# The first 8 MB of a streaming row sum: one load, or two half loads from two issuing engines

## The chip, the cores and the metric

The kernel runs on one core of one Trainium2 chip. The metric is the device time of one execution in microseconds (us). The span in a profile is some 1.4 us shorter than that execution's time (159.6 against 160.96 us for the kernel before).

Engines in the profile: ACT is ScalarE, DVE is VectorE, POOL is GpSimd, SP is SyncE, which only issues DMAs here. SPq and ACTq are the issuing instructions of SyncE and ScalarE. TensorE isn't used.

## The reference

```python
x = np.random.randn(32, 512, 1024).astype(np.float32)   # 67.11 MB
relu_x = np.maximum(x, 0)
return np.sum(relu_x, axis=-1).astype(np.float32)       # 64 KB
```

## The kernel before

The input is cut into eight portions of 16 rows on each of 128 partitions, 8.389 MB each. Seven are loaded whole into three buffers in turn, the eighth in smaller loads at the end. In the early portions ScalarE clamps a whole tile in place and VectorE sums its rows; towards the end both do single rows with clamp and sum in one instruction. `TWO` lists the row groups of each portion that are clamped and then summed. Lines that only count loads and semaphores are cut here.

```python
ROWS = 16
NBUF = 3
TWO = [[16], [16], [16], [8, 8], [8, 8], [7, 7], []]
# ...
def load(dst, src, after=None):
    dma = nc.sync.dma_start(out=dst, in_=src)
    if after:
        dma.wait_op(sems.dve, after[1], "sem-ge")     # the sum that frees the buffer
    dma.then_inc(sems.loads[n_load], 16)
# ...
for j in range(NB):
    buf = bufs[j % NBUF]
    loaded = load(buf[:, :, :], rows(m, ROWS), j >= NBUF and freed[j - NBUF])
    c = 0
    act_waits = dve_waits = loaded
    for n in TWO[j]:
        clamp(buf[:, c : c + n, :], act_waits)        # ScalarE, Relu in place
        total(buf[:, c : c + n, :], m + c, n)         # VectorE, sum of each row
        act_waits = None
        c += n
    # ... single rows of the later portions
    freed.append((n_act, n_dve))
```

A last function takes away the barrier that opens a program and moves the first load to the front, so that it is SyncE's first instruction (`EARLY = 1`).

Of the kernel before, what the change touches and what calls it, by code (L numbers as in the profile page):

```python
# [9 lines left out]
ROWS = 16  # L10
NBUF = 3


TWO = [[16], [16], [16], [8, 8], [8, 8], [7, 7], []]
ACT = [0, 0, 0, 0, 0, 2, 9]
DVE = [0, 0, 0, 0, 0, 0, 7]

# [2 lines left out]
TAIL = [8, 4]  # L20
START_PIECE, END_PIECE = 280, 260
PIECES = [240, 244]

EARLY = 1


def kernel(tc: tile.TileContext, x: bass.AP, out: bass.AP):
    nc = tc.nc
    sems = Semaphores(tc)

    tc.close()
    tc.compile()
    nc.cur_bb = nc.bb_map[tc.start_bb_name]
    body = nc.cur_bb.bb.instructions
    ends = list(body)
    body.clear()
    n_stores = relu_sum(nc, sems, x, out)
    body.extend(ends)


    nc.cur_bb = nc.bb_map[tc.start_bb_name + "_end"]
    nc.cur_bb.bb.instructions.clear()
    nums = sorted(s.num for s in (*sems.loads, sems.act, sems.dve))
    cleared = range(nums[0], nums[-1] + 1)
    assert len(cleared) == len(nums)
    nc.sync.sem_clear(cleared)
    nc.sync.wait_ge(sems.stored, 16 * n_stores).then_inc(sems.stored, -16 * n_stores)
    open_without_barrier(tc, EARLY)


class Semaphores:
    def __init__(self, tc: tile.TileContext):
        n = len(TWO) + len(TAIL) + 2 + len(PIECES)
        self.loads = [tc.alloc_semaphore(f"load{i}") for i in range(n)]
        self.act = tc.alloc_semaphore("act")
        self.dve = tc.alloc_semaphore("dve")
        self.stored = tc.alloc_semaphore("stored")


def relu_sum(nc, sems: Semaphores, x: bass.AP, out: bass.AP):  # L60
    x_flat = x.flatten_outer_dims()
    N, D = x_flat.shape
    NT = N // P
    NB = len(TWO)
    assert N == P * NT == P * ROWS * (NB + 1)
# [19 lines left out]
    def rows(m, n):  # L85
        if m < ROWS:
            return xf[:, m : m + n, :]
        return xv[:, m - ROWS : m - ROWS + n, :]
# [5 lines left out]

    n_load = n_act = n_dve = n_store = 0

    def load(dst, src, after=None):
        nonlocal n_load
        dma = nc.sync.dma_start(out=dst, in_=src)  # L99
        if after:  # L100
            dma.wait_op(sems.dve, after[1], "sem-ge")
        dma.then_inc(sems.loads[n_load], 16)
        n_load += 1
        return sems.loads[n_load - 1]
# [10 lines left out]
    def clamp(ap, loaded):  # L115
        nonlocal n_act
        i = nc.scalar.activation(out=ap, in_=ap, func=RELU)  # L117
        if loaded is not None:
            i.wait_op(loaded, 16, "sem-ge")
        i.then_inc(sems.act, 1)  # L120
        n_act += 1

    def total(ap, m, n):
        nonlocal n_dve
        nc.vector.tensor_reduce(  # L125
            out=res[:, m : m + n], in_=ap, axis=mybir.AxisListType.X, op=ADD
        ).wait_op(sems.act, n_act, "sem-ge").then_inc(sems.dve, 1)
        n_dve += 1

    def act_row(ap, accum_out, loaded):  # L130
        nonlocal n_act
        i = nc.scalar.activation(out=ap, in_=ap, func=RELU, accum_out=accum_out)  # L132
        if loaded is not None:
            i.wait_op(loaded, 16, "sem-ge")
        i.then_inc(sems.act, 1)
        n_act += 1

    def dve_row(ap, accum_out, loaded):
        nonlocal n_dve
        i = nc.vector.tensor_scalar(  # L140
            out=ap,
            in0=ap,
            scalar1=0.0,
            scalar2=None,
            op0=MAX,
            op1=ADD,
            accum_out=accum_out,
        )
        if loaded is not None:
            i.wait_op(loaded, 16, "sem-ge")  # L150
        i.then_inc(sems.dve, 1)
        n_dve += 1

    freed = []
    m = 0
    for j in range(NB):
        buf = bufs[j % NBUF]
        loaded = load(buf[:, :, :], rows(m, ROWS), j >= NBUF and freed[j - NBUF])
        c = 0
        act_waits = dve_waits = loaded  # L160
        for n in TWO[j]:
            clamp(buf[:, c : c + n, :], act_waits)
            total(buf[:, c : c + n, :], m + c, n)
            act_waits = None
            c += n
        for _ in range(ACT[j]):
            act_row(buf[:, c, :], res[:, m + c : m + c + 1], act_waits)
            act_waits = None
            c += 1
        for _ in range(DVE[j]):  # L170
            dve_row(buf[:, c, :], res[:, m + c : m + c + 1], dve_waits)
            dve_waits = None
            c += 1
        assert c == ROWS
        freed.append((n_act, n_dve))
        m += ROWS


    buf = bufs[NB % NBUF]
    c = 0  # L180
    for n in TAIL:
        loaded = load(
            buf[:, c : c + n, :], rows(m, n), None if c else freed[NB - NBUF]
        )
        for i in range(n):
            if i % 2 == 0 or (n == 8 and i == 7):
                act_row(buf[:, c, :], res[:, m : m + 1], loaded if i == 0 else None)
            else:
                dve_row(buf[:, c, :], res[:, m : m + 1], loaded if i == 1 else None)
            c += 1  # L190
            m += 1

    flat = buf[:, :, :].rearrange("p c d -> p (c d)")
    src = rows(m, 4).rearrange("p c d -> p (c d)")
    at = c * D
# [3 lines left out]
    last, w = parts[-1], PIECES[-1]  # L199
    others = [last[:, w + i : w + i + 1] for i in range(extra)]  # L200
    loaded = load(flat[:, at : at + b], src[:, :b])
    act_row(buf[:, c, :], res[:, m : m + 1], loaded)
    sums_act = n_act
# [3 lines left out]
    loaded = load(flat[:, at + end : at + 4 * D], src[:, end:])  # L207
# [13 lines left out]
    for i in range(len(PIECES) - 1):  # L221
# [3 lines left out]
        out=last[:, :],  # L225
# [9 lines left out]
    return n_store  # L235


def open_without_barrier(tc: tile.TileContext, n_loads: int):



    SP = mybir.EngineType.SP
    blocks = tc.nc.main_func.blocks
    opening = blocks[0].instructions
    body = next(b for b in blocks if b.name == tc.start_bb_name).instructions
    for i in list(opening):
        if isinstance(i, (mybir.InstDrain, mybir.InstEventSemaphore)):
            opening.remove(i)
    loads = [i for i in body if i.engine == SP][:n_loads]
    for i in loads:  # L250
        assert isinstance(i, mybir.InstDMACopy)
        body.remove(i)
    at = next(n for n, i in enumerate(opening) if i.engine == SP)
    opening[at:at] = loads


# [28 lines left out]
```

## Time and profile before

| | before |
|---|---|
| time, median of 6 runs | 161.07 us (160.96 to 161.15) |
| span of the profiled run | 159.6 us |
| DMA packets, share of 16 engines' span | 98.0% |
| VectorE busy, ScalarE busy | 74%, 65% |
| start of the clamps of loads 1, 2, 3 | 21.87, 41.19, 60.55 us |

How to read it: a clamp that starts just as its load lands, after a long idle time of ScalarE, is a mark for the landing. If the marks stand evenly 19.35 us apart, the stream of bytes has no gap, and only what lies ahead of the stream and behind it can be changed without moving fewer bytes. The prediction shows these lines.

### The profile page before, as it was taken

What the parts mean: (1) busy time and instruction counts of PE and PEld (TensorE: products, weight loads), DVE (VectorE), ACT (ScalarE), POOL (GpSimd) and SP (SyncE); (2) the same over time, 40 slices, a digit from 0 to 9 for tenths busy, and PEclk for the clock granted to TensorE, in tenths of its full rate; (3) what the DMA queues carried; (4) which work ended last, traced back from release to release, by engine and by line L of the source; (5) the groups of instructions that cost most, each with busy time, mean ns of one, the idle gap of its engine ahead of it and who ended that gap; (6) DMA issues with size and microseconds to landing.
All of it is one profiled execution on the core that took longest, in us unless ns stands there. A gap on an engine that the chain in (4) does not pass through costs nothing.

```text
span 159.6 us, 120 instructions
## 1 busy us (share of the span) xinstructions
DVE 117.6 (74%) x43; ACT 104.2 (65%) x50; POOL 0.2 (0%) x4
## 2 busy tenths in 40 slices
DVE  0000000009999499994999999999999999999986
ACT  3000059990699708996099951999329993499995
POOL 0000000000000000000000000000000000000000
DMA  7996996996997999979979969969969969798993
GB/s 279 509 526 263 526 526 263 526 509 279 526 476 312 526 394 394 526 345 443 526 328 460 526 263 526 526 263 526 509 279 526 493 296 526 337 452 382 418 412 119
DMA packets 2304, 67.18 MB, mean 421 GB/s; under 512 B 640, under 2 KB 896, under 8 KB 1024
## 3 DMA queue, kind: packets, MB, share of 16 engines
q1 hardware_dynamic: 2304, 67.18, 98.0%
HBM read 67.11 MB, written 0.07 MB: 421 GB/s over the span
## 4 chain that ended last, share of the span: by engine, by line
DMA 43%; DVE 34%; ACT 17%; another core or an unknown queue 3%; SPq 1%; issue 0%
DMA io<-in_x_dram 43%; DVE res L125 32%; ACT io L117 17%; DVE io L140 1%; SPq L99 1%; DVE piece L224 0%; DVE piece L140 0%
## 5 line engine op out<-in xcount | busy, mean ns | idle before, releaser
L125 DVE TENSOR_REDUCE res<-io 128x8 f32<-128x8192 f32 (+2 forms) x9 | 101.1, 11287 | 40.0 <-ACT io L117 40.0
L117 ACT ACTIVATE io<-io 128x8192 f32<-128x8192 f32 (+2 forms) x9 | 81.7, 9110 | 47.7 <-DMA io<-in_x_dram 47.7
L132 ACT ACTIVATE io<-io 128x1024 f32<-128x1024 f32 x20 | 20.9, 1045 | 6.0 <-DMA io<-in_x_dram 6.0
L140 DVE TENSOR_SCALAR_CACHE_REDUCE io<-io 128x1024 f32<-128x1024 f32 (+2 forms) x15 | 15.8, 1110 | 0.5 <-DMA io<-in_x_dram 0.4
L132 ACT ACTIVATION_READ_ACCUMULATOR io<-io 128x1 f32 x20 | 3.8, 188 | 0.0
L117 ACT ACT_TABLE_LOAD x1 | 1.3, 1283 | 0.1
L140 DVE DVE_READ_ACCUMULATOR io<-io 128x1 f32 x15 | 1.2, 82 | 0.0
L224 DVE TENSOR_SCALAR_CACHE_REDUCE piece<-piece 128x247 f32<-128x247 f32 x1 | 0.4, 410 | 0.0
L140 DVE TENSOR_SCALAR_CACHE_REDUCE piece<-piece 128x240 f32<-128x240 f32 x1 | 0.4, 397 | 0.0
L269 POOL MEMSET const-bfloat16-1.0<- 128x1 bf16 x1 | 0.1, 101 | 0.0
L269 POOL MEMSET const-uint8-127<- 128x1 uint8 x1 | 0.1, 101 | 0.0
L269 POOL MEMSET const-float32-0.0<- 128x1 f32 x1 | 0.1, 98 | 0.2 <-issue 0.2
L269 POOL MEMSET const-float32-1.0<- 128x1 f32 x1 | 0.1, 98 | 0.0
L224 DVE DVE_READ_ACCUMULATOR piece<-piece 128x1 f32 x1 | 0.1, 83 | 0.0
L140 DVE DVE_READ_ACCUMULATOR piece<-piece 128x1 f32 x1 | 0.1, 82 | 0.0
## 6 DMA issues: line engine op xcount, KB each, us to landing
io<-in_x_dram SPq DMA_DIRECT2D x1, 4096.0 KB, 21.6
io<-in_x_dram SPq DMA_DIRECT2D x1, 2048.0 KB, 26.1
io<-in_x_dram SPq DMA_DIRECT2D x1, 1164.0 KB, 28.4
io<-in_x_dram SPq DMA_DIRECT2D x1, 642.0 KB, 29.5
piece<-in_x_dram SPq DMA_DIRECT2D x1, 122.0 KB, 29.2
piece<-in_x_dram SPq DMA_DIRECT2D x1, 120.0 KB, 29.4
io<-in_x_dram SPq DMA_DIRECT2D x7, 26.9
out_dram<-res SPq DMA_DIRECT2D x1, 55.0 KB, 1.6
```

The costliest lines, as they stand in the source:

```text
L99: dma = nc.sync.dma_start(out=dst, in_=src)
L117: i = nc.scalar.activation(out=ap, in_=ap, func=RELU)
L125: nc.vector.tensor_reduce(out=res[:, m : m + n], in_=ap, axis=mybir.AxisListType.X, op=ADD).wait_op(sems.act, n_act, "sem-ge").then_inc(se ...
L132: i = nc.scalar.activation(out=ap, in_=ap, func=RELU, accum_out=accum_out)
L140: i = nc.vector.tensor_scalar(out=ap, in0=ap, scalar1=0.0, scalar2=None, op0=MAX, op1=ADD, accum_out=accum_out,)
L224: nc.vector.tensor_scalar(out=last[:, :], in0=last[:, :], scalar1=0.0, scalar2=None, op0=MAX, op1=ADD, accum_out=res[:, NT - 2 : NT - 1],) ...
L269: nc = _bacc.Bacc("TRN2", target_bir_lowering=False, num_devices=1)
```

## The change

The first portion comes as two loads of 8 rows a partition, one issued by SyncE and one by ScalarE, each moved to the front of its engine's program. The two halves are clamped and summed separately. The intent: start the transfer from two places at once, and start computing on half of the data. The core of the diff (counts of semaphores and unchanged lines cut):

```diff
-TWO = [[16], [16], [16], [8, 8], [8, 8], [7, 7], []]
+TWO = [[8, 8], [16], [16], [8, 8], [8, 8], [7, 7], []]
...
-EARLY = 1
+HALF = 8
...
-    def load(dst, src, after=None):
+    def load(dst, src, after=None, by=nc.sync):
         nonlocal n_load
-        dma = nc.sync.dma_start(out=dst, in_=src)
+        dma = by.dma_start(out=dst, in_=src)
...
-        loaded = load(buf[:, :, :], rows(m, ROWS), j >= NBUF and freed[j - NBUF])
+        if j == 0:
+            loaded = load(buf[:, :HALF, :], rows(m, HALF))
+            other = load(buf[:, HALF:, :], rows(m + HALF, ROWS - HALF), by=nc.scalar)
+        else:
+            loaded = load(buf[:, :, :], rows(m, ROWS), j >= NBUF and freed[j - NBUF])
+            other = None
...
-            act_waits = None
+            act_waits, other = other, None
...
-    loads = [i for i in body if i.engine == SP][:n_loads]
-    for i in loads:
-        assert isinstance(i, mybir.InstDMACopy)
-        body.remove(i)
-    at = next(n for n, i in enumerate(opening) if i.engine == SP)
-    opening[at:at] = loads
+    for engine in (mybir.EngineType.SP, mybir.EngineType.Activation):
+        first = next(i for i in body if isinstance(i, mybir.InstDMACopy) and i.engine == engine)
+        body.remove(first)
+        at = next(n for n, i in enumerate(opening) if i.engine == engine)
+        opening.insert(at, first)
```

## The prediction

> **What bounds the kernel now.** I began with the chain that ended last and the busy table of the page. They show DVE 74% busy, ACT 65%, and a chain that jumps between loads, clamps and sums. That chain must not be taken at its word, so the next view was the DMA queue, then the order of time for ACT and DVE, then how many bytes the DMA engines took up in short windows at the start.
>
> From the page (the queue, then the chain as shares of the span):
>
> ```profile
> DVE 117.6 (74%) x43; ACT 104.2 (65%) x50; POOL 0.2 (0%) x4
> q1 hardware_dynamic: 2304, 67.18, 98.0%
> DMA 43%; DVE 34%; ACT 17%; another core or an unknown queue 3%; SPq 1%; issue 0%
> ```
>
> The second line says that packets fill 98.0% of 16 DMA engines' whole span. No compute engine comes near that.
>
> From the timeline (start, duration, engine and line, what it did, and in brackets the idle time before it with what ended it):
>
> ```profile
> 21.87 13.86 ACT L117 ACTIVATE io<-io 128x16384 f32<-128x16384 f32 x1 [20.47 <-DMA io<-in_x_dram]
> 35.76 17.22 DVE L125 TENSOR_REDUCE res<-io 128x16 f32<-128x16384 f32 x1 [35.76 <-ACT io L117]
> 41.19 13.86 ACT L117 ACTIVATE io<-io 128x16384 f32<-128x16384 f32 x1 [5.46 <-DMA io<-in_x_dram]
> 55.08 17.22 DVE L125 TENSOR_REDUCE res<-io 128x16 f32<-128x16384 f32 x1 [2.10 <-ACT io L117]
> 60.55 13.86 ACT L117 ACTIVATE io<-io 128x16384 f32<-128x16384 f32 x1 [5.50 <-DMA io<-in_x_dram]
> ...
> 118.60 12.24 ACT L117 ACTIVATE io<-io 128x7168 f32<-128x7168 f32 x2 [5.40 <-DMA io<-in_x_dram]
> ...
> 137.96 1.06 ACT L132 ACTIVATE io<-io 128x1024 f32<-128x1024 f32 x1 [5.04 <-DMA io<-in_x_dram]
> ```
>
> ACT waits about 5.5 us for every 8 MB load, and its starts mark the landings: 21.87, 41.19, 60.55. The steps are 19.32 and 19.36, and from 118.60 to 137.96 again 19.36. A load is 128 x 16 x 1024 x 4 bytes = 8.389 MB, so the stream runs at 8.389 MB / 19.35 us = 433.5 GB/s without a gap. The input is 67.11 MB, eight such portions, 154.8 us. The span is 159.6 us, so 4.8 us are outside the stream: 21.84 - 19.35 = 2.5 us ahead of it, and about 2.3 us behind it (last sums, store).
>
> The DMA row of the chain, 28.43 us from 126.91 to 155.34, holds mostly queueing: that load was issued when a sum of rows ended at 126.04, while the load before it was still on its way until 137.9. Its wait had 11.9 us to spare. For the fourth load the same: it waits for the sum that ends at 35.76 + 17.22 = 52.98, and the third load lands only at 60.5, 7.5 us later. So no buffer wait ever starves the queue.
>
> The start, in windows (width, DVE, ACT, POOL busy, clock, DMA packet time per engine as a share of the window and counted at the packet's start, GB/s likewise):
>
> ```profile
> 0.00:1.00 1.00, 0.00 (x0) 0.88 (x1) 0.20 (x4) 1.00 0.00 0
> 1.00:2.00 1.00, 0.00 (x0) 0.40 (x1) 0.00 (x0) 1.00 3.01 1049
> 2.00:3.50 1.50, 0.00 (x0) 0.00 (x0) 0.00 (x0) 1.00 0.00 0
> 3.50:5.00 1.50, 0.00 (x0) 0.00 (x0) 0.00 (x0) 1.00 1.61 699
> 5.00:6.00 1.00, 0.00 (x0) 0.00 (x0) 0.00 (x0) 1.00 0.00 0
> 6.00:7.00 1.00, 0.00 (x0) 0.00 (x0) 0.00 (x0) 1.00 2.42 1049
> ```
>
> 1049 GB/s in a window of 1 us is 1.049 MB, exactly 16 packets of 64 KB, one for each DMA engine. So all first packets start between 1.0 and 2.0 us and last 3.01 us on average; the second ones, between 3.5 and 5.0 us, last 1.61 x 1.5 = 2.42 us, and the third ones 2.42 us too. From the packet records the first 64 KB packet starts at 1.01 us, the sixteenth at 1.81, the mean at 1.24; the second packets start at 3.96 to 4.58. So the 2.5 us ahead of the stream are some 1.24 us until the mean engine has data to move, 3.01 - 2.42 = 0.59 us of a slow first packet, 4.58 - 4.25 = 0.33 us by which the slowest engine trails the mean (the starts of the last engine trail the mean just so in all later rows), and about 0.3 us until the last semaphore is seen.
>
> **What the Trainium skill says.** "DMA: Bandwidth & Descriptors", section "Issuing engines are not separate DMA queues": DMAs from different engines run on the same 16 DMA engines and interleave; using several saves only the time to initiate them. Here an issue takes 0.38 us on SyncE (its first row in the chain), and nothing yet shows two queues at once. The same page, "Queues, rings and completion order": each DMA engine goes round-robin between the queue rows at packet granularity, so two halves issued together should end together and not one after the other; the trace of before has one queue and can't say. Same page, "Where 436 GB/s comes from": a ceiling of 435.2 GB/s at the SBUF ports, with about 358 named as binding for HBM reads; the trace disagrees with the second and comes within 0.4% of the first at 433.5. Same page, "Latency and other measured facts": first byte after about 600 ns on this path; here the first packet starts 1.01 us after the issue begins, of which 0.38 is the issue, which leaves 0.63 and agrees.
>
> **The change part by part.**
>
> *Two half loads in place of the first.* The bytes are the same, 4.19 MB each, and so is the stream's rate. The packets are 32 KB, an estimate of 1.21 us each at the present rate. They alternate between the rings on every engine. SyncE's own next load (8 MB) stands behind its half, so no engine runs dry. I expect both halves to land at nearly the same time, around 20.5 to 22 us. Nothing is gained in the stream itself: 0.
>
> *Time to the first packet.* SyncE's load already was the first instruction of the program, so its first packet stays at about 1.0 us: 0. ScalarE's earliest work now is a table load at 0.12 us; its DMA takes that place, so its half is queued about 0.1 us after SyncE's. It costs ACT some 0.4 us and pushes the 1.28 us table load to an end near 1.9 us, 19 us before its first clamp: off the path.
>
> *The slow first packet and the engine lag.* This is the one place with something to win, at most 0.59 + 0.33 = 0.92 us. A second ring may overlap the slow opening with the other ring's, or the two rings may both have slow first packets in turn (up to another 0.59 us lost). I choose a gain of 0.15 us, a small part of the first, as nothing in the trace says what the 0.59 us are.
>
> *First buffer's compute.* One clamp of 13.86 us becomes two of 7.02 (the later 8-row ones last that long; two together 13.95), one sum of 17.22 becomes two of 8.68. The first sum can start at 21.9 + 7.0 = 28.9 in place of 35.8, the second ends near 46.2 in place of 52.98. That frees the first buffer about 6.8 us earlier and the fourth load is issued so much earlier, but it then waits behind the third load till 60.5 as before. DVE idles up to 55.1 in both. Gain: 0.
>
> *Semaphore.* One more to clear at the end: under 0.1 us.
>
> Sum: 161.07 - 0.15 = 160.9 us. As every later landing comes so much earlier, ACT and DVE behind it shift as a whole: DVE runs without a break from 74.44, which was itself released by the clamp of the load that landed at 60.5.
>
> **Rivals.** *The earlier sum as a real gain.* Speaking for it: 6.8 us of DVE waiting vanish, and the chain gives DVE 34%. Against it: the DMA row of 98.0% and 7.5 us of spare time at the buffer's wait. If it were right the time would be near 154 us, but 154.8 us of stream alone forbid that. *Starting the stream much sooner.* Even if all 2.5 us before it vanished, the time would be 158.6, 1.6% less; that bounds the gain under 2%. A full removal of slow packet and lag gives 160.2. *Interference of two queues.* If alternating rings or 32 KB packets cost 5% of the first 19.35 us, the time rises by 1.0 us to 162.0; 2% slower (3.2 us) would need 17% there. Against it: the tail of the kernel has small packets too and the windows from 147.0 to 155.3 still show 415 GB/s. *A late ScalarE queue.* If its half came 5 us late, only the second clamp would wait, and DVE has 9 us to spare: the time stays.
>
> **Range and chances.** The effect I count is 0.15 us, with a possible 0.9 us each way where the start is unclear; runs of the same kernel spread by 0.1 us. So 160.3 to 161.5 should hold it 8 times in 10. Beyond 2% either way, no mechanism that I found reaches: 1% for faster, 1% for slower, left for what I can't see.
>
> **What would show it.** Right: packets of the first 8 MB on two queues, 32 KB each; first ones at about 1.0 us; the two halves land within some 1.5 us of each other near 21.5; ACT still waits over 5 us for each 8 MB load with landings 19.35 us apart; DVE's first sum near 29 us; the buffer's third use still without effect on landings; the queue still 98%. Wrong: landings after the first that have moved by over 0.6 us against before, a step between landings other than 19.35, first packets well before 1.0 us, or a longer time with the stream unchanged, which would be a cost ahead of the first or behind the last instruction.

## More of the kernel before

All runs here are of state fast, with a granted clock of 1.0.

The experiments were taken on three chips, each time with the kernel before beside them (its medians were 161.09, 161.03 and 161.06 us).

## The result, and the profile after

The changed kernel takes 161.09 us (160.95 to 161.21, 6 runs) against 161.07 us of the kernel before, ratio 1.0001 with a 95% interval of 0.9988 to 1.0014: the same. A ratio here is the mean time of one kernel's fast runs over that of the other's of the same rounds, so it is not quite the ratio of the medians that are quoted.

The queues on the page of the changed kernel (queue, kind, packets, MB, share of 16 engines' span):

```profile
q1 hardware_dynamic: 2304, 62.98, 91.9%
q10 hardware_dynamic: 144, 4.19, 6.1%
```

ScalarE's half is 4.19 MB on a queue of its own; the sum of the shares, 98.0%, is that of before.

The timeline of the changed kernel's start:

```profile
0.12 0.37 ACTq L100 DMA_DIRECT2D io<-in_x_dram  x1
...
0.52 1.28 ACT L118 ACT_TABLE_LOAD   x1 [0.52 <-issue]
21.80 13.95 ACT L118 ACTIVATE io<-io 128x8192 f32<-128x8192 f32 x2 [20.00 <-DMA io<-in_x_dram]
28.87 17.28 DVE L126 TENSOR_REDUCE res<-io 128x8 f32<-128x8192 f32 x2 [28.87 <-ACT io L118]
41.17 13.86 ACT L118 ACTIVATE io<-io 128x16384 f32<-128x16384 f32 x1 [5.41 <-DMA io<-in_x_dram]
55.05 17.22 DVE L126 TENSOR_REDUCE res<-io 128x16 f32<-128x16384 f32 x1 [8.91 <-ACT io L118]
60.51 13.86 ACT L118 ACTIVATE io<-io 128x16384 f32<-128x16384 f32 x1 [5.49 <-DMA io<-in_x_dram]
...
118.57 12.24 ACT L118 ACTIVATE io<-io 128x7168 f32<-128x7168 f32 x2 [5.40 <-DMA io<-in_x_dram]
...
137.92 1.06 ACT L133 ACTIVATE io<-io 128x1024 f32<-128x1024 f32 x1 [5.03 <-DMA io<-in_x_dram]
```

The first sum starts at 28.87 us in place of 35.76, and the first buffer's sums end at 28.87 + 17.28 = 46.15 in place of 52.98. But the clamp of the second load starts at 41.17 in place of 41.19, and so on down to 137.92 in place of 137.96. VectorE's gain went into a longer idle time: 8.91 us before the sum at 55.05, where it was 2.10.

The same is to be read in SyncE's waits for VectorE (total, how often, the longest). First the kernel before, then the changed one:

```profile
SPq L99 <- DVE res L125: 123.3, 5, 51.7
```

```profile
SPq L100 <- DVE res L126: 123.3, 5, 44.8
```

The longest wait, that of the fourth load for the first buffer, is 6.9 us shorter. The total is 123.3 us in both: what SyncE wins at its first wait it spends at the next ones, as the sums behind are bound to landings that haven't moved.

The windows of the changed kernel's start (columns as in the prediction):

```profile
0.00:1.00 1.00, 0.00 (x0) 0.48 (x1) 0.20 (x4) 1.00 0.00 0
1.00:2.00 1.00, 0.00 (x0) 0.80 (x1) 0.00 (x0) 1.00 1.77 524
2.00:3.50 1.50, 0.00 (x0) 0.00 (x0) 0.00 (x0) 1.00 0.81 350
3.50:5.00 1.50, 0.00 (x0) 0.00 (x0) 0.00 (x0) 1.00 0.81 350
```

524 GB/s in 1 us are 16 packets of 32 KB, one for each DMA engine. They start between 1 and 2 us as before and last 1.77 us on average; the next sixteen last 0.81 x 1.5 = 1.21 us. The packet records say that the first sixteen are SyncE's, the next sixteen ScalarE's (starting at 2.80 to 3.28 us), and so on in turn. The slow opening costs 1.77 - 1.21 = 0.56 us, where one load paid 3.01 - 2.42 = 0.59. It is paid once, by the first queue; ScalarE's first packets last 1.21 us, as if they were in the middle of a stream. The last engine finishes its first 64 KB at 4.49 us instead of 4.58, and the later landings come 0.02 to 0.04 us earlier. Neither is clear of the spread between profiles. In five kernels below and above that open with the same single load, that engine finishes at 4.58 to 4.79 us and the second load's clamp starts at 41.19 to 41.40; in the four that open with two half loads, from one queue or two, at 4.42 to 4.58 and at 41.11 to 41.25. So the opening may gain 0.1 to 0.2 us, with one queue as well as with two, but the ranges meet or overlap and the times do not resolve it: such a gain is not shown.

### The profile page after: what moved, and what is told of

Read it like the earlier page. It is cut to its first block, busy times and chain, and to the rows that moved or that the text cites. A ratio compares the mean times of both kernels' runs of the same rounds, so it can differ in the third digit from the quotient of the medians.

```text
span 159.6 us, 123 instructions
## 1 busy us (share of the span) xinstructions
DVE 117.7 (74%) x44; ACT 104.3 (65%) x51; POOL 0.2 (0%) x4
## 3 DMA queue, kind: packets, MB, share of 16 engines
q10 hardware_dynamic: 144, 4.19, 6.1%
## 4 chain that ended last, share of the span: by engine, by line
DMA 43%; DVE 34%; ACT 17%; another core or an unknown queue 3%; SPq 1%; issue 0%
DMA io<-in_x_dram 43%; DVE res L126 32%; ACT io L118 17%; DVE io L141 1%; SPq L100 1%; DVE piece L230 0%; DVE piece L141 0%
## 5 line engine op out<-in xcount | busy, mean ns | idle before, releaser
L133 ACT ACTIVATE io<-io 128x1024 f32<-128x1024 f32 x20 | 20.9, 1043 | 6.0 <-DMA io<-in_x_dram 6.0
## 6 DMA issues: line engine op xcount, KB each, us to landing
io<-in_x_dram ACTq DMA_DIRECT2D x1, 4096.0 KB, 21.8
```

Of the source, the lines that this page charges most:

```text
L133: i = nc.scalar.activation(out=ap, in_=ap, func=RELU, accum_out=accum_out)
```

## The experiments

Ten kernels ran, all with right results but for one that was meant to be wrong.

| kernel | time, median | ratio to the kernel before |
|---|---|---|
| both halves from SyncE | 161.05 | 0.9998 (0.9981 to 1.0016) |
| one load, compute split 8 and 8 | 161.12 | 0.9999 (0.9983 to 1.0014) |
| 1 row, then 15 rows | 161.59 | 1.0029 (1.0012 to 1.0045) |
| hardly any work on the first buffer (wrong result) | 161.02 | 0.9992 (0.9976 to 1.0008) |
| kernel before, first load issued 2.7 us late | 163.83 | 1.0175 (1.0161 to 1.0189) |
| changed kernel, SyncE's half issued 2.9 us late | 161.18 | 1.0009 (0.9996 to 1.0021) |
| two buffers, kernel before | 197.52 | 1.2266 |
| two buffers, changed kernel | 190.50 | 1.1830 |
| two buffers, one load, compute split | 190.57 | 1.1832 |
| two buffers, both halves from SyncE | 190.14 | 1.1801 |

My theory was that the stream of packets sets the end, so the change can act only through the moment at which the stream starts. The rivals: the earlier sum and the earlier free buffer are worth something, or the second queue helps or disturbs.

### The second queue taken away

```diff
-            other = load(buf[:, HALF:, :], rows(m + HALF, ROWS - HALF), by=nc.scalar)
+            other = load(buf[:, HALF:, :], rows(m + HALF, ROWS - HALF))
-    for engine in (mybir.EngineType.SP, mybir.EngineType.Activation):
+    for engine in (mybir.EngineType.SP,):
```

> The change with both halves issued by SyncE, one behind the other, at the head of the program. My theory (the stream of packets sets the end, the first packet starts at 1.0 us after SyncE's first issue whatever stands behind it): 161.1 us, ratio 1.000 within 0.002. The halves land one after the other, near 11.8 us and 21.6 us, DVE's first sum starts near 18.8 us (28.9 in the changed kernel), ACT's clamp of the second load still starts near 41.2. Rival 1, the second queue does something (helps or disturbs): this run differs from the changed kernel by 0.3 us or more. Rival 2, an earlier first sum pays: this run has it 10 us earlier still and is faster by several us.

161.05 us, ratio 0.9998. The timeline of this kernel:

```profile
12.04 7.03 ACT L118 ACTIVATE io<-io 128x8192 f32<-128x8192 f32 x1 [10.64 <-DMA io<-in_x_dram]
19.10 8.69 DVE L126 TENSOR_REDUCE res<-io 128x8 f32<-128x8192 f32 x1 [19.10 <-ACT io L118]
21.76 7.03 ACT L118 ACTIVATE io<-io 128x8192 f32<-128x8192 f32 x1 [2.69 <-DMA io<-in_x_dram]
...
41.11 13.86 ACT L118 ACTIVATE io<-io 128x16384 f32<-128x16384 f32 x1 [12.32 <-DMA io<-in_x_dram]
```

From one queue the halves land one after the other, at 12.0 and 21.8 us. From two queues they land together: in the changed kernel's packet records the last semaphore packets of the two halves are 0.01 us apart, at 21.4 us, because the two queues' rings (each queue's own list of packets at a DMA engine) alternate packet by packet: through both halves the records have sixteen packets of one queue, then sixteen of the other. So for getting the first rows early, the second queue does harm: the first sum starts at 28.87 with two queues and at 19.10 with one. Neither matters to the end.

### Only the compute split

```diff
-TWO = [[16], [16], [16], [8, 8], [8, 8], [7, 7], []]
+TWO = [[8, 8], [16], [16], [8, 8], [8, 8], [7, 7], []]
```

> The kernel before with its one first load, only the first clamp and sum split 8 and 8. My theory: first sum at about 28.9 us in place of 35.8, first buffer free near 46.2 in place of 53.0, and the time stays at 161.1, ratio 1.000 within 0.002, since the fourth load then queues 14 us in place of 7.5. Rival, the earlier release pays: up to 6.8 us faster.

161.12 us, ratio 0.9999; the sums of the first buffer run from 29.04 to 46.32 us. The earlier release is worth nothing by itself. The second load's clamp starts 0.11 us later than in the kernel before, which opens with the same load; that is spread between profiles:

```profile
41.30 13.86 ACT L117 ACTIVATE io<-io 128x16384 f32<-128x16384 f32 x1 [5.37 <-DMA io<-in_x_dram]
```

### Hardly any work on the first buffer

```diff
-            clamp(buf[:, c : c + n, :], act_waits)
-            total(buf[:, c : c + n, :], m + c, n)
+            w = 64 if j == 0 else D
+            clamp(buf[:, c : c + n, :w], act_waits)
+            total(buf[:, c : c + n, :w], m + c, n)
```

> Wrong result on purpose: first clamp and sum work on 64 of 1024 columns, so 13 us of ACT and 16 us of DVE vanish from the first buffer and it is free near 25 us in place of 53. My theory: 161.1 us, ratio 1.000 within 0.002; landings of all later loads unchanged. Rival, the first buffer's compute or its release is on the path that sets the end: faster by 5 us or more.

161.02 us, ratio 0.9992. With 16 us of VectorE's work and nearly 13 us of ScalarE's gone, and the buffer free at 24.4 us, the clamp of the second load starts at 41.40:

```profile
41.40 13.86 ACT L117 ACTIVATE io<-io 128x16384 f32<-128x16384 f32 x1 [18.27 <-DMA io<-in_x_dram]
```

So no shortening of the first buffer's compute can be seen in the time. The rival of the earlier sum falls, for this kernel.

### The start moved on purpose

Six tiny loads (64 bytes on each of 16 partitions, into a tile that nobody reads) go ahead of SyncE's first load, in the kernel before and in the changed one.

```diff
+    for i in range(LATE):                      # LATE = 6
+        cols = slice(16 * i, 16 * i + 16)
+        nc.sync.dma_start(out=idle[:, cols], in_=x_flat[:16, cols]).then_inc(sems.loads[-1], 16)
...
-EARLY = 1
+EARLY = 1 + LATE
```

> The kernel before with six tiny loads (64 bytes on each of 16 partitions) issued by SyncE ahead of the first load; each takes SyncE about 0.45 us, so the first load is issued 2.7 us later. My theory (the start of the stream is on the path one to one): landings and end 2.7 us later, 163.8 us within 0.4. Rival, the start has slack: 161.1.

> The changed kernel with the same six tiny loads ahead of SyncE's half. My theory: ScalarE's half starts the stream at 0.12 + 1.0 us and alone fills the 16 DMA engines until SyncE's half joins at 3.7 us, so the end stays within 0.4 us of 161.1, and the slow first packet (1.8 us for 32 KB in place of 1.21) is now on ScalarE's queue. So the second issuer is worth the whole delay of the first, which in the kernel before is nothing. Rival, one queue with 32 KB packets cannot fill the engines, or ScalarE's queue starts slower: 162.5 to 163.8.

The kernel before takes 163.83 us, 2.80 more than the 161.03 of its rounds; the changed kernel 161.18. The timelines, the kernel before with its late start first:

```profile
0.00 2.69 SPq L158 DMA_DIRECT2D idle<-in_x_dram  x6
...
2.74 72.71 SPq L100 DMA_DIRECT2D io<-in_x_dram  x5
24.64 13.86 ACT L118 ACTIVATE io<-io 128x16384 f32<-128x16384 f32 x1 [23.23 <-DMA io<-in_x_dram]
...
43.99 13.86 ACT L118 ACTIVATE io<-io 128x16384 f32<-128x16384 f32 x1 [5.50 <-DMA io<-in_x_dram]
```

```profile
0.00 2.84 SPq L159 DMA_DIRECT2D idle<-in_x_dram  x6
0.12 0.38 ACTq L101 DMA_DIRECT2D io<-in_x_dram  x1
...
2.88 69.88 SPq L101 DMA_DIRECT2D io<-in_x_dram  x5
21.93 13.95 ACT L119 ACTIVATE io<-io 128x8192 f32<-128x8192 f32 x2 [20.11 <-DMA io<-in_x_dram]
...
41.30 13.86 ACT L119 ACTIVATE io<-io 128x16384 f32<-128x16384 f32 x1 [5.41 <-DMA io<-in_x_dram]
```

A load that is issued 2.74 us later lands 2.77 us later (24.64 against 21.87), so does the next (43.99 against 41.19), and the end is 2.80 us later: the start of the stream counts one to one. In the changed kernel ScalarE's half alone keeps the 16 DMA engines busy from 1.1 us on, and SyncE's delay is gone from the time. That is what the second issuer can give: it covers a late first one. One part of the expectation was wrong: SyncE's half did not join at 3.7 us. By the packet records its first bulk packets start only at 11.43 us, when all of ScalarE's half has been taken up. Until then its tiny packets (64 bytes, and 4 bytes for each semaphore) stand ahead of it on its ring, and from 4.8 us on sixteen of them start for every sixteen 32 KB packets of ScalarE. So here a packet took a turn however small it was. In the kernel before nothing is late, as SyncE's load already is the first instruction of the program.

### A small first load

```diff
-TWO = [[8, 8], [16], ...
+TWO = [[1, 15], [16], ...
-HALF = 8
+HALF = 1            # and both loads from SyncE, as above
```

> First load 1 row a partition (4 KB packets), then 15 rows (60 KB packets), both from SyncE. It asks what the slow first packet is. Theory a, a fixed latency of each DMA engine's first packet, as 3.01 - 2.42 = 0.59 us and 1.77 - 1.21 = 0.56 us for 64 KB and 32 KB suggest: the 4 KB packets average 0.15 + 0.57 = 0.7 us for the first on each engine and the 60 KB packets come at their steady 2.27 us. Theory b, a slow stretch of time (the first 3 us of reading run slow): first 4 KB packets about 0.2 to 0.3 us, and the early 60 KB packet is slow by the rest of 0.57. Both leave the time at 161.1 within 0.3 us, as the 0.57 us is only moved; a gain of 0.5 us would say that a small first packet removes it.

161.59 us, ratio 1.0029: 0.5 us slower, outside what I had written for both theories. The first 4 KB packets last 0.78 us on average, about as the first theory has it, but they range from 0.16 to 1.36, and the next sixteen still take 0.26 us in place of 0.16. By the packet records, the 60 KB packets start between 2.96 and 3.83 us. In the kernel before, the last engine has its first 32 KB at about 4.58 - 1.21 = 3.37 us (half a packet back from its second packet's start; up to 3.58 in the other profiles with that opening); here at 3.83, 0.25 to 0.46 us later. The clamp of the second load starts at 41.70, 0.30 to 0.51 us later than in those kernels, and by its interval the end is 0.2 to 0.7 us later. So here a lag of the first 4 us stays to the end, and a small first load made it bigger; why, no run shows.

### What the slow first packet is

The late start answers this too. In it, each DMA engine had carried six tiny packets before its first 64 KB packet. A window of that kernel:

```profile
3.00:4.80 1.80, 0.00 (x0) 0.00 (x0) 0.00 (x0) 1.00 1.70 583
```

1.70 x 1.80 us is 3.06 us of packet time per engine, one 64 KB packet (3.04 by the records) and tiny ones. The slow packet is still there, though it is no engine's first. My theory of a latency that each engine pays once, with its first packet, falls. With two buffers, the queue runs dry in the middle of the kernel. A window of the two-buffer kernel before, where the stream starts again after 13 us without packets:

```profile
54.00:55.00 1.00, 0.00 (x0) 1.00 (x1) 0.00 (x0) 1.00 3.13 1049
```

Again sixteen packets of 64 KB, at 3.13 us each. All seven restarts in the two-buffer kernels before and after (after 5.5 to 13.1 us without packets) have first packets of 2.95 to 3.22 us on average, followed by 2.42. So 0.5 to 0.8 us on average came with every start of the bulk stream seen here, at the beginning or later, and a queue that joined a running stream didn't pay it (1.21 us for ScalarE's first packets in the changed kernel, and for SyncE's at 11.43 us above).

Nor is it a fixed price for each engine. In the changed kernel the first packets that start at 1.01 to 1.11 us last 1.79 to 2.08 us, and the last of the sixteen, which starts at 1.85, lasts 1.21, the steady time. With both halves from SyncE, those that start at 1.75 and 1.99 us last 1.21 as well. That looks like a slow stretch of time that the engines share, but no run was made to test it, and what happens in it inside the memory or the DMA engine, no run here shows.

### A third buffer taken away

If the earlier release is real but hidden, it must show where the buffers are scarce. Both kernels with two buffers in place of three; the sixth portion is done 8 and 8, so that the wait for the buffer covers all readers.

```diff
-NBUF = 3
+NBUF = 2
-TWO = [..., [7, 7], []]
-ACT = [0, 0, 0, 0, 0, 2, 9]
+TWO = [..., [8, 8], []]
+ACT = [0, 0, 0, 0, 0, 0, 9]
```

> The kernel before with two buffers of 16 rows in place of three (and the sixth load's rows done 8 and 8 with none on ScalarE alone, for the buffer's wait to cover all). Now the third load waits for the first sum, with only the second load in the queue till 41.2 us: the DMA queue runs dry. Estimate from the durations of the profile: span 193 us, time 194.5, within 4.

> The changed kernel with the same two buffers. My theory: the earlier release of the first buffer (46.2 in place of 53.0 us) is real but hidden by the third buffer; with two it shows: third load issued 6.8 us earlier, end about 7 us earlier than the two-buffer kernel before, 187.5 us within 4, ratio of the two about 0.963. Rival, the split brings nothing of its own or is given back at the next wait for a buffer (fourth load waits for the second sum at 72.3 us in both): ratio within 0.01 of 1.

197.52 and 190.50 us: 7.0 us less, ratio of the medians 0.964. The estimates were 3 us low for both. My working had given a load into a dry queue 20.9 us from issue to landing; the chain below has 21.77, or 0.87 more. The kernel before has three such loads, so this may be about 2.6 us of its miss; that of the changed kernel was not taken apart. The chain that ended last in the two-buffer kernel before (start, duration, what):

```profile
35.87 17.23 DVE res L125
53.10 0.02 issue
53.12 21.77 DMA io<-in_x_dram
74.89 0.02 issue
```

The same view of the two-buffer changed kernel:

```profile
41.25 13.87 ACT io L118
55.11 0.02 issue
55.14 17.23 DVE res L126
72.37 0.02 issue
72.39 21.94 DMA io<-in_x_dram
```

In the first the third load is issued by the sum that ends at 53.10; the first buffer is on the path. In the second that wait is shorter and another one sets the end: the fourth load waits for the second buffer, at 72.37. Here a DMA row of the chain is to be believed, since the queue is empty when the load is issued.

Two more kernels ask which part of the change gives the 7 us (edits as above, in the two-buffer kernel).

> Two buffers, one first load from SyncE, only the first clamp and sum split 8 and 8. Theory: the 7.0 us that two buffers showed come from splitting the compute (first sum starts with half the rows), not from the second issuer; then this equals the two-buffer changed kernel, 190.5 us within 0.4, third load issued near 46.3. Rival, the two queues or the two landings carry the gain: 197.5.

> Two buffers, both halves from SyncE one behind the other. Buffer 0 is free near 37.6, before the second load lands at 41.2, so the queue does not run dry there and the third load lands near 60.5 in place of 68.3. But the even loads gain what the odd ones cannot use: the fourth load still waits for the second sum (72.3), the sixth for the sum that ends near 118.7, the last ones for 164.8. Theory: the end is set by that odd chain, 190.4 us within 0.6. Rival, the earlier landing passes through: 183 to 184 us.

190.57 us with only the compute split: the split of clamp and sum gives the whole gain, the two loads and the second issuer none. 190.14 us with both halves from one queue: although the third load lands at 60.50 in place of 68.26, 7.8 us earlier, only 0.4 us pass through, because the end hangs on the other buffer's chain; its fourth load is still issued at 72.28. So it is in part chance that a release 6.9 us earlier gave just 7.0: in the changed kernel the sixth load would land near 140.5 us by either chain (121.10 us for the fifth load's clamp and 19.35 behind it, or 118.72 for the issue and 21.8 from a dry queue), so a still earlier release has hardly more to give.

No kernel beat the kernel before: of those with a right result, the fastest median lies 0.04 us under that of its rounds, with an interval that holds 1.

## Why the prediction was right

- **What bounds the kernel.** Right. 433.5 GB/s without a gap; taking the first buffer's work away changes nothing, and moving the start by 2.74 us moves the end by 2.80.
- **First buffer's compute, gain 0.** Right in each number: first sum at 28.87 (28.9 predicted), sums end at 46.15 (46.2), fourth load issued 6.9 us earlier (6.8), landings unmoved. With two buffers the earlier release is worth 7.0 us, so the mechanism exists and the third buffer hides it.
- **The halves land together.** Right, 0.01 us apart.
- **Time to the first packet.** Right: 1.01 us after SyncE's issue in both. ScalarE's DMA starts at 0.12 us and the table load ends at 1.80 (1.9 predicted), without effect: ScalarE then waits another 20.0 us for its first clamp (the prediction's 19 is a slip of its sum).
- **The slow first packet and the lag, a gain of 0.15 us.** This term was chosen, not worked out, and the runs do not settle its size. The second queue did not overlap the slow opening, which was one of the two ways that the prediction saw, nor pay it again, which was the other: ScalarE's packets stood behind SyncE's slow ones (2.80 us and later) and then took 1.21 us each. The opening cost 0.56 us against 0.59, and between profiles it varies from 0.49 to 0.74 with two half loads and from 0.51 to 0.67 with one. In time, the interval of 0.9988 to 1.0014 is about 0.2 us each way and holds a gain of 0.15 as well as none, so 161.09 is no test of it. The wide range carried this term: 161.09 lies inside 160.3 to 161.5.
- **Interference of two queues.** Didn't happen. The packets of 32 KB last 1.21 us on either ring, half of 2.42. What the prediction cites on several issuers, that they save only the time to initiate, held: 161.18 against 163.83 us where SyncE was late, nothing where it wasn't.

## What to carry to other kernels

Look first whether the landings are evenly spaced at the stream's rate; if they are, an earlier sum or an earlier free buffer only turns into idle time elsewhere, and the chain's rows of computing are no promise. Then ask what starts the stream: a second issuing engine is worth about what the first one is late (2.65 of 2.80 us here, the one delay tried), which is nothing when its load is already its first instruction. For the first rows to arrive early, queue the parts behind each other on one queue (the first half was there at 12.0 us, the second at 21.8); from two queues they arrived together, at 21.8.

## What the Trainium skill lacked or had wrong

- "DMA: Bandwidth & Descriptors", "Latency and other measured facts", has a first-byte latency but not the slow start of the stream: the engines' first 64 KB packets last 3.01 us on average in place of 2.42 at the beginning, and 2.95 to 3.22 at all seven restarts after a dry spell; a second queue that joined a running stream didn't pay it (1.21 us for 32 KB from its first packet). I found it on no other page that I read.
- The same page, "Where 436 GB/s comes from", says that the HBM side, with about 358 GB/s for a core, binds transfers between HBM and SBUF, though it also has 425 GB/s measured for a 16 MB load. The whole stream here ran at 433.5 GB/s on one core, near the 435.2 of the ports, so the sentence about what binds does not hold for a kernel like this one. The runs do not record what the other cores did.
